# Binary cross-entropy on one core: target as u8, longer rows, one software DMA queue, a small first tile and a last tile in pieces

## The chip, the cores and the metric

The kernel runs on one core of a Trainium2 chip. The metric is the device time of one execution in microseconds (us), lower is better. Before the change it is 1882.6 us (median of 4 runs, 1882.17 to 1883.1).

## The reference

```python
pred   = uniform(0.01, 0.99, (8192, 8192)) as float32
target = randint(0, 2, (8192, 8192)) as float32      # 0.0 or 1.0
pred = clip(pred, 1e-7, 1 - 1e-7)
out  = -(target * log(pred) + (1 - target) * log(1 - pred))
```

Because target is 0 or 1, each output is one of two logarithms, negated. Both inputs and the output are 268.4 MB in DRAM, so 805.3 MB have to cross between DRAM and the core. No kernel here can avoid that.

## The kernel before

```python
W = n_cols                      # 8192
C = 2048
p_pool = tile_pool(bufs=4)      # [128, 8192] fp32
t_pool = tile_pool(bufs=4)      # [128, 8192] bf16
u_pool = tile_pool(bufs=2, space=PSUM)

for rb in range(num_row_blocks):            # 64
    # ... cut: allocation of p_tile and t_tile
    nc.gpsimd.dma_start(out=p_tile, in_=pred_f[r0:r1, :])
    nc.gpsimd.dma_start(out=t_tile, in_=target_f[r0:r1, :])   # casts fp32 to bf16
    for cb in range(num_chunks):            # 4 chunks of 2048
        # ... cut: c0, c1, u_tile
        nc.scalar.activation(u_tile, p_tile[:, c0:c1], LN, bias=0.0, scale=1.0)
        nc.scalar.activation(p_tile[:, c0:c1], p_tile[:, c0:c1], LN, bias=1.0, scale=-1.0)
        nc.vector.copy_predicated(out=p_tile[:, c0:c1],
                                  mask=t_tile[:, c0:c1].bitcast(i16), data=u_tile)
        nc.vector.tensor_scalar_mul(out=p_tile[:, c0:c1], in0=p_tile[:, c0:c1], scalar1=-1.0)
    nc.scalar.dma_start(out=out_f[r0:r1, :], in_=p_tile)
```

ScalarE makes log(pred) into PSUM, the second on-chip memory beside that of the tiles, and log(1 - pred) in place. VectorE overwrites the latter with the former where target is 1, then negates. The loads go through GpSimd's software queue, the stores through ScalarE's hardware queue.

## Time and profile before

| | before |
|---|---|
| span of the profiled execution | 1880.6 us |
| VectorE / ScalarE busy | 49% / 51% |
| DMA queues, share of 16 engines | 66.6% loads, 33.2% stores |
| one row's DMA record: pred / target / store | 1213 / 1227 / 1213 to 1226 ns |
| rate in the bulk, counted in DRAM bytes | 432.7 GB/s |
| DMA idle: first 10 us / after 1800 us | 2.8 / 13.8 us |

A row is what one DMA record of the trace moves: 8192 elements of one partition, 32,768 B on the DRAM side. The row times are the usual values of such records. The bulk is the stretch from 200 to 1800 us; its rate gives each row its DRAM bytes, spread over its record, in stretches of 150 us. Idle is the mean over 16 engines of the time with fewer than 16 records in flight, up to the end of the last record.

From the page of the kernel before: the DMA line of the 40-slice part (each digit is the busy share of a slice in tenths), the queues (packets, MB, share), and the engines and lines of the chain that ended last.

```profile
DVE 923.0 (49%) x512; ACT 951.5 (51%) x513; POOL 72.2 (4%) x132
...
DMA  9999999999999999999999999999999999999996
...
q0 software_dynamic: 18432, 402.66, 66.6%
q10 hardware_dynamic: 9216, 268.44, 33.2%
...
another core or an unknown queue 44%; ACT 38%; DVE 12%; issue 3%; DMA 2%; POOL 0%; ACTq 0%; DVEq 0%; PEldq 0%
```

DMA is saturated everywhere but in the last slice, and no compute engine is busy for more than 51% of the span. The two shares stand as 2 to 1, as the loads' DRAM bytes do to the stores'. The 402.66 MB of the first queue are written bytes, where target counts only half. So the time follows the side with more bytes.

The waits of the kernel before (engine, line, what was waited for: us in total, times, longest):

```profile
POOL p_tile L48 <- DMA out_dram<-p_tile: 1598.3, 56, 57.1
DVE p_tile L60 <- ACT p_tile L57: 834.4, 88, 14.8
ACT u_tile L56 <- DMA p_tile<-in_pred_dram: 799.2, 63, 14.6
```

Everybody waits for transfers: the loads for a store to free a buffer, ScalarE for pred, VectorE for ScalarE. These waits cost nothing while the DMA engines have work. What costs is where the engines run out of work. Two stretches of the kernel before, by engine busy time, clock, DMA share and GB/s (written bytes):

```profile
200.00:1800.00 1600.00, 795.16 (x441) 816.78 (x441) 58.57 (x109) 1.00 1.01 360
...
1845.00:1881.00 36.00, 14.66 (x8) 14.83 (x8) 0.00 (x0) 1.00 0.56 238
```

At the end, 0.44 of 36 us, 16 us, are idle, the last store's completion included. The timeline there (start, duration, instruction, idle before it and what ended it):

```profile
1839.54 1.23 DVE L63 TENSOR_SCALAR p_tile<-p_tile 128x2048 f32<-128x2048 f32 x1
1849.19 1.88 ACT L56 ACTIVATE u_tile<-p_tile 128x2048 f32<-128x2048 f32 x1 [12.71 <-DMA p_tile<-in_pred_dram]
1851.10 1.91 ACT L57 ACTIVATE p_tile<-p_tile 128x2048 f32<-128x2048 f32 x1
1851.11 0.34 ACTq L67 DMA_DIRECT2D out_dram<-p_tile  x1
...
1867.90 0.34 ACTq L67 DMA_DIRECT2D out_dram<-p_tile  x1
```

The next-to-last block is finished at 1840.8, but its store leaves ScalarE's queue at 1851.1, behind the first logarithm of the last block. The last store leaves at 1867.9, once all four chunks are done.

### The profile page before, as it was taken

The numbers are of one execution on the slowest core, as the hardware profiler recorded it, in microseconds if no ns is written. First come the engines' busy times: TensorE is split into PE (matmuls) and PEld (weight loads), VectorE is DVE, ScalarE is ACT, GpSimd is POOL, SyncE is SP. The second block draws the span as 40 slices with busy tenths as digits, with TensorE's granted clock in tenths as the row PEclk, the third lists the DMA queues.
The fourth block names the chain that finished last, engine by engine and source line by source line (L and its number), as shares of the span: only waits on it lengthen the run. The fifth ranks groups of instructions, "written<-read, shape, count | busy, mean of one in ns | idle before, by whom it ended". The sixth has DMA issues, their size and how long they took to land.

```text
span 1880.6 us, 1631 instructions
## 1 busy us (share of the span) xinstructions
DVE 923.0 (49%) x512; ACT 951.5 (51%) x513; POOL 72.2 (4%) x132
## 2 busy tenths in 40 slices
DVE  3545535446354464454544545536355354563544
ACT  4545545546445455464553644635446455464453
POOL 0000000000000000000000000000000000000000
DMA  9999999999999999999999999999999999999996
GB/s 309 373 357 351 338 356 373 345 377 356 351 378 345 365 366 347 384 344 355 378 343 375 355 350 383 344 363 370 343 382 350 351 381 345 370 361 346 385 345 286
DMA packets 27661, 671.21 MB, mean 357 GB/s; under 512 B 3072, under 2 KB 3072, under 8 KB 3072
## 3 DMA queue, kind: packets, MB, share of 16 engines
q0 software_dynamic: 18432, 402.66, 66.6%
q10 hardware_dynamic: 9216, 268.44, 33.2%
q14 instruction: 13, 0.11, 0.0%
HBM read 536.87 MB, written 268.44 MB: 428 GB/s over the span
## 4 chain that ended last, share of the span: by engine, by line
another core or an unknown queue 44%; ACT 38%; DVE 12%; issue 3%; DMA 2%; POOL 0%; ACTq 0%; DVEq 0%; PEldq 0%
ACT u_tile L56 20%; ACT p_tile L57 18%; DVE p_tile L60 11%; DMA t_tile<-in_target_dram 2%; DVE p_tile L63 1%; POOL p_tile L48 0%; ACTq L56 0%; POOL t_tile L49 0%; DVEq L60 0%; PEldq L93 0%
## 5 line engine op out<-in xcount | busy, mean ns | idle before, releaser
L60 DVE COPY_PREDICATED p_tile<-t_tile,u_tile 128x2048 f32<-128x2048 int16 x256 | 619.3, 2432 | 938.3 <-ACT p_tile L57 834.4
L56 ACT ACTIVATE u_tile<-p_tile 128x2048 f32<-128x2048 f32 x256 | 479.2, 1872 | 902.9 <-DMA p_tile<-in_pred_dram 799.2
L57 ACT ACTIVATE p_tile<-p_tile 128x2048 f32<-128x2048 f32 x256 | 484.9, 1906 | 9.0 <-DVE p_tile L63 2.9
L63 DVE TENSOR_SCALAR p_tile<-p_tile 128x2048 f32<-128x2048 f32 x256 | 310.6, 1224 | 6.6
L48 POOL DMA_DIRECT2D p_tile<-in_pred_dram x64 | 35.5, 555 | 1708.2 <-DMA out_dram<-p_tile 1598.3
L49 POOL DMA_DIRECT2D t_tile<-in_target_dram x64 | 37.3, 583 | 7.4 <-DVE p_tile L60 7.3
L56 ACT ACT_TABLE_LOAD x1 | 1.3, 1283 | 0.7 <-PEq L82 0.7
L82 POOL MEMSET const-float32-0.0<- 128x1 f32 x1 | 0.1, 98 | 0.2 <-issue 0.2
L82 POOL MEMSET const-bfloat16-1.0<- 128x1 bf16 x1 | 0.1, 101 | 0.0
L82 POOL MEMSET const-float32-1.0<- 128x1 f32 x1 | 0.1, 98 | 0.0
L82 POOL MEMSET const-uint8-127<- 128x1 uint8 x1 | 0.1, 98 | 0.0
## 6 DMA issues: line engine op xcount, KB each, us to landing
p_tile<-in_pred_dram POOLq DMA_DIRECT2D x64, 4096.0 KB, 61.6
out_dram<-p_tile ACTq DMA_DIRECT2D x64, 4096.0 KB, 23.1
t_tile<-in_target_dram POOLq DMA_DIRECT2D x64, 2048.0 KB, 75.7
```

Of the source, the lines that this page charges most:

```text
L48: nc.gpsimd.dma_start(out=p_tile, in_=pred_f[r0:r1, :])
L49: nc.gpsimd.dma_start(out=t_tile, in_=target_f[r0:r1, :])
L56: nc.scalar.activation(u_tile, p_tile[:, c0:c1], LN, bias=0.0, scale=1.0)
L57: nc.scalar.activation(p_tile[:, c0:c1], p_tile[:, c0:c1], LN, bias=1.0, scale=-1.0)
L60: nc.vector.copy_predicated(out=p_tile[:, c0:c1], mask=t_tile[:, c0:c1].bitcast(i16), data=u_tile)
L63: nc.vector.tensor_scalar_mul(out=p_tile[:, c0:c1], in0=p_tile[:, c0:c1], scalar1=-1.0)
L82: nc = _bacc.Bacc("TRN2", target_bir_lowering=False, num_devices=1)
```

## The change

Its intent is to move the same bytes in fewer, longer rows and to leave less work for the ends. The core of the diff, condensed (`...` and the comment lines stand for code that is cut, and some lines are shortened):

```diff
-    bf16 = mybir.dt.bfloat16
+    u8 = mybir.dt.uint8
-    C = 2048 if n_cols % 2048 == 0 else n_cols
+    CH = 1888
+    C = 8 * CH                                       # 15104: rows of 60,416 B
+    # flat view: widths = [1888] + [15104] * 34 + [8864], 36 tiles
-    p_pool = ... bufs=4;  t_pool = ... bufs=4;  u_pool = ... bufs=2 (2048 wide)
+    p_pool = ... bufs=3;  t_pool = ... bufs=2;  u_pool = ... bufs=1 (3776 wide)
+    # u_pool becomes bufs=2, 1888 wide, for the last two tiles
     ...
+    p_load_split(0, engine=nc.sync)                  # small first tile
+    t_load(0); p_load(1); t_load(1); p_load(2)       # all on gpsimd
+    for k in range(NT):
+        # chunks of 3776 (1888 in the last two tiles): ln, ln, copy_predicated, negate
-                out=p_tile[:, c0:c1], mask=t_tile[:, c0:c1].bitcast(i16), data=u_tile
+                out=p_tile[:, c0:c1], mask=t_tile[:, c0:c1], data=u_tile[:, 0:cw]
+            if last: nc.sync.dma_start(out=dr_out[:, c0:c1], in_=p_tile[:, c0:c1])
-        nc.scalar.dma_start(out=out_f[r0:r1, :], in_=p_tile)
+        store(k)                                     # on gpsimd
+        t_load(k + 2)
+        p_load(k + 3)
```

The loads, formerly issued at the head of each block and prefetched by the pools alone, are now placed by hand behind the store.

More of the change, by code (lines that the diff above doesn't have):

```diff
@@ L18 @@
     P = nc.NUM_PARTITIONS
+    fp32 = mybir.dt.float32
+    u8 = mybir.dt.uint8
+    LN = mybir.ActivationFunctionType.Ln
     pred_f = pred.flatten_outer_dims()
-    target_f = target.flatten_outer_dims()
-    out_f = out.flatten_outer_dims()
     n_rows, n_cols = pred_f.shape
-    assert n_rows % P == 0
-    fp32 = mybir.dt.float32
-    bf16 = mybir.dt.bfloat16
-    i16 = mybir.dt.int16
-    LN = mybir.ActivationFunctionType.Ln
-    W = n_cols
-    C = 2048 if n_cols % 2048 == 0 else n_cols
-    num_row_blocks = n_rows // P
@@ L35 @@
-    num_chunks = W // C
-    p_pool = ctx.enter_context(tc.tile_pool(name="p_pool", bufs=4))
-    t_pool = ctx.enter_context(tc.tile_pool(name="t_pool", bufs=4))
-    u_pool = ctx.enter_context(tc.tile_pool(name="u_pool", bufs=2, space=bass.MemoryType.PSUM))
-    for rb in range(num_row_blocks):
-        r0 = rb * P
-        r1 = r0 + P
-        p_tile = p_pool.tile([P, W], fp32)
-        t_tile = t_pool.tile([P, W], bf16)
-        nc.gpsimd.dma_start(out=p_tile, in_=pred_f[r0:r1, :])
-        nc.gpsimd.dma_start(out=t_tile, in_=target_f[r0:r1, :])
-        for cb in range(num_chunks):
-            c0 = cb * C
-            c1 = c0 + C
-            u_tile = u_pool.tile([P, C], fp32)
-            nc.scalar.activation(u_tile, p_tile[:, c0:c1], LN, bias=0.0, scale=1.0)
+    N = n_rows * n_cols
@@ new lines @@
+    assert N % P == 0
+    F = N // P
+    pf = pred.flatten()
+    tf = target.flatten()
+    of = out.flatten()
+    CH = 1888
+    C = 8 * CH
+    if F <= C:
+        C = F
+        CH = min(2048, C)
+        widths = [C]
+    else:
+        C0 = CH
+        rem = F - C0
+        n_full = rem // C
+        tail = rem - n_full * C
+        widths = [C0] + [C] * n_full + ([tail] if tail else [])
+    NT = len(widths)
+    offs = [0] * NT
+    for k in range(1, NT):
+        offs[k] = offs[k - 1] + P * widths[k - 1]
@@ new lines, with dram_tile_full @@
+    p_bufs = min(3, NT)
+    t_bufs = min(2, NT)
+    p_pool = ctx.enter_context(tc.tile_pool(name="p_pool", bufs=p_bufs))
+    t_pool = ctx.enter_context(tc.tile_pool(name="t_pool", bufs=t_bufs))
+    u_ctx = ExitStack()
+    u_pool = u_ctx.enter_context(tc.tile_pool(name="u_wide", bufs=1, space=bass.MemoryType.PSUM))
+    p_tiles: dict[int, object] = {}
+    t_tiles: dict[int, object] = {}
+    def dram_tile_full(flat_ap, k):
+        base = offs[k]
+        w = widths[k]
+        return flat_ap[base : base + P * w].rearrange("(p c) -> p c", c=w)
@@ new lines, in p_load, with p_load_split @@
+    def p_load(k, engine=None):
+        w = widths[k]
+        tl = p_pool.tile([P, C], fp32, name="ptile")
+        (engine or nc.gpsimd).dma_start(out=tl[:, 0:w], in_=dram_tile_full(pf, k))
+        p_tiles[k] = tl
+    def p_load_split(k, engine, p_split=32):
+        w = widths[k]
+        tl = p_pool.tile([P, C], fp32, name="ptile")
+        src = dram_tile_full(pf, k)
+        engine.dma_start(out=tl[0:p_split, 0:w], in_=src[0:p_split, :])
+        engine.dma_start(out=tl[p_split:P, 0:w], in_=src[p_split:P, :])
+        p_tiles[k] = tl
@@ new lines, in t_load, with store @@
+    def t_load(k):
+        w = widths[k]
+        tl = t_pool.tile([P, C], u8, name="ttile")
+        nc.gpsimd.dma_start(out=tl[:, 0:w], in_=dram_tile_full(tf, k))
+        t_tiles[k] = tl
+    def store(k):
+        w = widths[k]
+        eng = nc.gpsimd
+        eng.dma_start(out=dram_tile_full(of, k), in_=p_tiles[k][:, 0:w])
+    if NT > 1:
+        p_load_split(0, engine=nc.sync)
+    else:
+        p_load(0)
+    for b in range(min(t_bufs, NT)):
+        t_load(b)
+        if b + 1 < min(p_bufs, NT):
+            p_load(b + 1)
@@ new lines @@
+    for k in range(NT):
+        p_tile = p_tiles[k]
+        t_tile = t_tiles[k]
+        ck = widths[k]
+        last = k == NT - 1
+        dr_out = dram_tile_full(of, k) if last else None
+        if k == NT - 2:
+            u_ctx.close()
+            u_pool = ctx.enter_context(tc.tile_pool(name="u_pool", bufs=2, space=bass.MemoryType.PSUM))
+        cmax = CH if k >= NT - 2 else 2 * CH
+        c0 = 0
+        while c0 < ck:
+            cw = min(cmax, ck - c0)
+            c1 = c0 + cw
+            u_tile = u_pool.tile([P, cmax], fp32, name="utile")
+            nc.scalar.activation(
+                u_tile[:, 0:cw], p_tile[:, c0:c1], LN, bias=0.0, scale=1.0
+            )
@@ L65 @@
             )
-        nc.scalar.dma_start(out=out_f[r0:r1, :], in_=p_tile)
+            if last and NT > 1:
+                nc.sync.dma_start(out=dr_out[:, c0:c1], in_=p_tile[:, c0:c1])
+            c0 = c1
+        if last:
+            if NT == 1:
+                store(k)
+            break
+        store(k)
+        if k + t_bufs <= NT - 1:
+            t_load(k + t_bufs)
+        if k + p_bufs <= NT - 1:
+            p_load(k + p_bufs)
 _INS = ['pred', 'target']
```

## The prediction

> **What bounds the kernel now.** The DMA engines. The slice row has DMA at 9 in every slice but the last; the queue table gives 66.6% of 16 engines' span to the software queue (loads) and 33.2% to the hardware queue (stores); VectorE is busy 49%, ScalarE 51%. In the waits, loads wait 1598 us for stores to land, ScalarE 799 us for pred. The chain of waits names 44% an unknown queue, which I read as the same thing.
>
> The bytes that count are those of the wider side. In the DMA records a 32,768 B pred row takes 1213 ns, a target row (32,768 B read, 16,384 B bf16 written) 1227 ns, a store row 1213 to 1226 ns. So the cast's smaller output buys nothing. From 200 to 1800 us there are 23,790 packets, 2,651 of them tiny completions: 21,139 rows x 32,768 B in 1600 us = 433 GB/s. The Trainium skill, "DMA: Bandwidth & Descriptors", section Bandwidth ("Where 436 GB/s comes from"), puts the ceiling at 435 GB/s; this trace agrees, 0.5% under. The 805.3 MB at 433 GB/s are 1861 us; the other 20 us are ends: 2 us before the first packet, about 16 us idle in the last 36 us (DMA share 0.56 in the window 1845 to 1881), because the last two 4 MB stores wait for whole-tile compute.
>
> **What the change does.** Target becomes u8 (still 4 B read per element). Rows grow from 32,768 to 60,416 B, 192 transfers become about 113. All bulk transfers go on one software queue, in the order store k, target k+2, pred k+3; buffers fall to 3 and 2. PSUM has one 3776-wide buffer, so ScalarE and VectorE hardly overlap. The first tile is small; the last is stored in pieces on another queue.
>
> **Costs, estimated from the durations above.**
> - DMA: per-row overhead (1213 against 1205 ns at 27.2 B/ns, the skill's ceiling) is paid half as often: about -5 us. With one queue nothing hides the cast's 14 ns per row and the completions: 0 to +8 us. Bulk 1860 to 1870 us.
> - Compute per 15,104-wide tile: 4 serial chunks of ln 3.4 + ln 3.4 + predicated copy 4.4 us (scaled from 1.87, 1.91 and 2.43 us at 2048), plus the last negation 2.2: 47 us. DMA per tile: 3 x 7.73 MB at 433 GB/s = 54 us. Compute stays hidden, 13% spare. The pred load waits for its store to land, but an 18 us target load is queued between, so the engines do not run dry.
> - Tail: queued transfers cover the last compute; idle in the last 36 us falls from 16 to about 3 us. Start: no change.
>
> **Predicted time: 1870 us, 8 in 10 within 1861 to 1882.** Faster by over 2%: 3%; within 2%: 92%; slower by over 2%: 5%. At 435 GB/s 805.3 MB are 1851 us, so 2% (1845 us) is out of reach unless something else binds.
>
> **What would show each step.** HBM bytes unchanged (537 read, 268 written); row records of about 2230 ns for pred, 2240 to 2260 for target; DMA 9 in all slices, the last no longer 6; ScalarE waiting for VectorE's predicated copy, both still near 50% busy; load waits still ended by stores landing.
>
> **What would make it wrong.** The cast to u8 running slower than the read side (each extra 100 ns per target row costs about 28 us); a u8 mask slowing the predicated copy so that a tile's chain passes 54 us; the single queue draining at tile boundaries, or reads and writes in turn running below 433 GB/s.

## The result

The changed kernel takes 1866.65 us (median of 8 runs, 1865.46 to 1869.63), against 1882.43 us (13 runs) for the kernel before. The ratio is 0.9916 with a 95% interval of 0.9906 to 0.9926. A ratio here is the mean time of one kernel's runs over that of the other's of the same rounds, so it is not quite the ratio of the medians quoted. Executions over 1.5% slower than the fastest of the same kernel are left out of the means. The gain of 15.8 us is clear of noise.

| | before | after |
|---|---|---|
| span of the profiled execution | 1880.6 us | 1865.3 us |
| row record: pred / target | 1213 / 1227 ns | 2229 / 2244 ns |
| bulk rate, DRAM bytes | 432.7 GB/s | 433.9 GB/s |
| DMA idle: first 10 us / after 1800 us | 2.8 / 13.8 us | 1.9 / 4.0 us |

From the page of the changed kernel, the same parts:

```profile
DVE 897.7 (48%) x292; ACT 928.9 (50%) x293; POOL 57.0 (3%) x110
...
DMA  9999999999999999999999999999999999999998
...
q0 software_dynamic: 15264, 598.48, 99.3%
q1 hardware_dynamic: 880, 5.51, 0.8%
...
ACT 36%; DVE 34%; another core or an unknown queue 26%; DMA 2%; issue 1%; DVEq 0%; POOL 0%; PEldq 0%
```

Still saturated, now also in most of the last slice. The chain of waits names ScalarE and VectorE for 70% of the span, and the engines are not busier: a chain is one path back through releases, and its shares are not costs. (The experiments e11 and e12 show how far compute is from binding.)

The waits of the changed kernel:

```profile
POOL ptile L69 <- DMA out_dram<-ptile: 1574.8, 33, 49.0
ACT utile L116 <- DVE ptile L122: 892.6, 134, 15.5
DVE ptile L122 <- DMA ttile<-in_target_dram: 476.3, 34, 29.2
```

ScalarE waiting for VectorE's predicated copy is now 892.6 us, against 103.7 in the kernel before: with one PSUM buffer, the next logarithm can start only when the copy has read the last one. Two stretches of the changed kernel:

```profile
200.00:1800.00 1600.00, 771.62 (x240) 795.18 (x242) 48.10 (x90) 1.00 1.00 325
...
1829.00:1866.00 37.00, 15.21 (x10) 9.39 (x6) 0.00 (x0) 1.00 0.82 337
```

The DMA share at the end is 0.82 in place of 0.56: 7 us idle, not 16. The 325 against 360 GB/s of the bulk is not a slowdown. It counts written bytes, and u8 writes fewer. The end of the changed kernel's timeline shows what is in flight:

```profile
1824.03 0.54 POOL L89 DMA_DIRECT2D out_dram<-ptile  x1 [39.07 <-DVE ptile L125]
1825.37 1.78 ACT L119 ACTIVATE ptile<-ptile 128x1888 f32<-128x1888 f32 x1
1835.92 4.39 DVE L122 COPY_PREDICATED ptile<-ttile,utile 128x1888 f32<-128x1888 uint8 x2 [12.18 <-DMA ttile<-in_target_dram]
...
1849.29 1.88 DVE L125 TENSOR_SCALAR ptile<-ptile 128x1888 f32<-128x1888 f32 x2
```

The next-to-last store (7.7 MB, about 18 us of transfer) is issued at 1824, before the last target has landed (1835.9). In the queue it stands right behind that load, and it runs while the last tile is computed: by the DMA records 102 of its 128 rows end after 1835.9, the last one at 1854.

### The profile page after: what moved, and what is told of

It is laid out like the page before. It is cut to its first block, busy times and chain, and to the rows that moved or that the text cites. A ratio compares the mean times of both kernels' runs of the same rounds, so it can differ in the third digit from the quotient of the medians.

```text
span 1865.3 us, 922 instructions
## 1 busy us (share of the span) xinstructions
DVE 897.7 (48%) x292; ACT 928.9 (50%) x293; POOL 57.0 (3%) x110
## 4 chain that ended last, share of the span: by engine, by line
ACT 36%; DVE 34%; another core or an unknown queue 26%; DMA 2%; issue 1%; DVEq 0%; POOL 0%; PEldq 0%
DVE ptile L122 32%; ACT ptile L119 18%; ACT utile L116 18%; DMA ttile<-in_target_dram 2%; DVE ptile L125 2%; DVEq L122 0%; DVEq L167 0%; POOL ttile L83 0%; POOL ptile L69 0%; PEldq L167 0%
## 5 line engine op out<-in xcount | busy, mean ns | idle before, releaser
L122 DVE COPY_PREDICATED ptile<-ttile,utile 128x3776 f32<-128x3776 uint8 (+1 forms) x146 | 602.5, 4129 | 948.6 <-DMA ttile<-in_target_dram 476.3
L116 ACT ACTIVATE utile<-ptile 128x3776 f32<-128x3776 f32 (+1 forms) x146 | 462.2, 3166 | 907.5 <-DVE ptile L122 892.6
L119 ACT ACTIVATE ptile<-ptile 128x3776 f32<-128x3776 f32 (+1 forms) x146 | 466.3, 3195 | 4.5
L125 DVE TENSOR_SCALAR ptile<-ptile 128x3776 f32<-128x3776 f32 (+1 forms) x146 | 296.2, 2031 | 4.9
L69 POOL DMA_DIRECT2D ptile<-in_pred_dram x35 | 18.6, 532 | 1574.8 <-DMA out_dram<-ptile 1574.8
L89 POOL DMA_DIRECT2D out_dram<-ptile x35 | 18.8, 536 | 191.7 <-DVE ptile L125 191.7
L83 POOL DMA_DIRECT2D ttile<-in_target_dram x36 | 19.7, 548 | 0.8 <-PEq L167 0.8
```

The costliest lines, as they stand in the source:

```text
L69: (engine or nc.gpsimd).dma_start(out=tl[:, 0:w], in_=dram_tile_full(pf, k))
L83: nc.gpsimd.dma_start(out=tl[:, 0:w], in_=dram_tile_full(tf, k))
L89: eng.dma_start(out=dram_tile_full(of, k), in_=p_tiles[k][:, 0:w])
L116: nc.scalar.activation(u_tile[:, 0:cw], p_tile[:, c0:c1], LN, bias=0.0, scale=1.0)
L122: nc.vector.copy_predicated(out=p_tile[:, c0:c1], mask=t_tile[:, c0:c1], data=u_tile[:, 0:cw])
```

## The experiments

The theory was: 11 us of the gain are idle time at the ends (16.6 to 5.9 us in the table), 5 us are the longer rows, and u8 by itself and the choice of queue are worth nothing. Its rivals: fewer bytes written on chip, the single queue, the stores in pieces. All kernels gave correct results.

### e1: the kernel before, stores from SyncE

```diff
-        nc.scalar.dma_start(out=out_f[r0:r1, :], in_=p_tile)
+        nc.sync.dma_start(out=out_f[r0:r1, :], in_=p_tile)
```

> The kernel before with one edit: the stores are issued from SyncE, not from ScalarE's queue. Theory (the gain of the change is 11 us of idle at the ends and some 5 us of larger rows): in the kernel before, the next-to-last store, though its data were negated by 1840.8 us, left ScalarE's queue only at 1851.1, behind the next tile's logarithms; freed of that, about 5 us of the idle at the end go: 1877 us (1875 to 1879), DMA in the bulk unchanged at 433 GB/s. Rival 1 (the cast to u8 or the row size alone makes the gain): 1882 us, no change. Rival 2 (late stores cost all through the run): well below 1875 us.

Measured: 1883.45 us (1881.03 to 1885.61), ratio 1.0005 (0.999 to 1.002). This is a miss: 1875 to 1879 was expected. The stores do leave at once, but the idle after 1800 us grew from 13.8 to 16.7 us. The timeline of e1 at the end:

```profile
1841.76 3.68 ACT L56 ACTIVATE u_tile<-p_tile 128x2048 f32<-128x2048 f32 x2 [3.21 <-DMA p_tile<-in_pred_dram]
1845.38 3.69 ACT L57 ACTIVATE p_tile<-p_tile 128x2048 f32<-128x2048 f32 x2
1857.64 4.74 DVE L60 COPY_PREDICATED p_tile<-t_tile,u_tile 128x2048 f32<-128x2048 int16 x2 [14.90 <-DMA t_tile<-in_target_dram]
```

The DMA engines keep the same rate in the bulk (432.7 GB/s in e1 too), so a store that runs earlier pushes the last load later. The last target now lands at 1857.6. In the kernel before, the last load to land was pred, at 1849.2. After it only the last block is left, and the DMA engines idle through its 14 us of compute. What matters at the end is not how early a store goes, but how much is still queued when the last load lands.

### e2: e1, and the last block stored chunk by chunk

```diff
+            if rb == num_row_blocks - 1:
+                nc.sync.dma_start(out=out_f[r0:r1, c0:c1], in_=p_tile[:, c0:c1])
...
-        nc.scalar.dma_start(out=out_f[r0:r1, :], in_=p_tile)
+        if rb < num_row_blocks - 1:
+            nc.sync.dma_start(out=out_f[r0:r1, :], in_=p_tile)
```

> The kernel before, stores from SyncE, and the last row block stored in four pieces as each 2048-wide chunk is done. Theory: the end's idle falls by about 10 us in all, 1871.5 us (1869 to 1874): more than half of the change's 15.8 us, without u8, larger rows or a single queue. Rival (the gain is in the bulk of the transfers): no more than e1.

Measured: 1878.65 us (1876.41 to 1880.27), ratio 0.9983 (0.9966 to 1.0). The idle after 1800 us fell to 4.3 us as expected, but the time fell by 3.7 us, not 11, and lies outside the 1869 to 1874 expected: a miss in size. In the profiled execution (span 1874.6 us) the rate sags to 429 to 431 GB/s from 1400 to 1850 us, which costs some of what the end gains. The times themselves spread by 4 us, where the kernel before spreads by 1.3. In its mechanism at the end the theory holds. The sag was not foreseen, and its cause stays open; 186 rows of this run take over 5% more than usual, against 50 in the kernel before, and e7 has more of this.

### e3: the kernel before, target as u8

```diff
-        t_tile = t_pool.tile([P, W], bf16)
+        t_tile = t_pool.tile([P, W], mybir.dt.uint8)
...
-mask=t_tile[:, c0:c1].bitcast(i16)
+mask=t_tile[:, c0:c1]
```

> The kernel before with one edit: target is cast to u8 in place of bf16, a quarter of the read size is written in place of half. Theory (a transfer takes the time of its wider, read side): 1882 us (1881 to 1884), target rows 1227 ns as before, HBM bytes the same. Rival (bytes written to on-chip memory count): 67 MB fewer, at 433 GB/s some 150 us off, or a part of that.

Measured: 1881.45 us, ratio 0.9995 (0.998 to 1.001). A target row takes 1227 ns, as with bf16, though it writes 8192 B in place of 16,384. By itself u8 is worth nothing that is clear of the noise: the median is 0.9 us lower, and the interval contains 1. It makes room on chip: at the changed kernel's tile width, bf16 has one more byte for each target element, which over two buffers of 15,104 elements would add 30 KB per partition.

### e4 and e6: the changed kernel with the old row size

```diff
-    CH = 1888
+    CH = 1024
```

> The changed kernel with chunk width 1024 in place of 1888, so rows of 32,768 B as before, all else kept. Theory (each row of 16 engines pays 8 to 10 ns beside its bytes, whatever its size, and the target rows some 14 ns more): row records 1213 and 1227 ns, bulk longer by about 8 us against the changed kernel: 1874 us (1871 to 1878). Rival (row size is worth nothing; the single queue or the order of transfers makes the bulk faster): 1866.7 us, as the changed kernel.

Measured in e4: 1872.83 us, but spread from 1870.32 to 1880.93. The profiled execution was the slowest of the four, with a bulk rate down to 423 GB/s in the middle. It was run again beside the changed kernel itself (e5), on one chip, with more rounds.

> The changed kernel itself, unaltered, as the control for the other runs of this group on the same chip. Both theories: 1866.7 us (1865 to 1870), a ratio of 0.9916 to the kernel before.

Measured in e5: 1866.27 us (1865.45 to 1866.96), ratio 0.9911.

> The kernel of e4 again, because e4's four times spread from 1870 to 1881 us and the rate of its profiled run dips to 423 GB/s for some 300 us in the middle. Theory (larger rows lift the bulk rate from 432.8 to 433.9 GB/s, some 5 us): fastest runs 1870 us, 4 to 6 us over the changed kernel's fastest, and the target of 433 GB/s in a run without a dip. Rival (row size is worth nothing, e4's median was disturbance): within 2 us of the changed kernel.

Measured in e6: 1871.31 us (1870.81 to 1875.04), ratio 0.9944 (0.9932 to 0.9956). The fastest runs differ by 5.4 us and the medians by 5.0. Rows are 1213 and 1227 ns again. The last stretch of e6, as long as that of the changed kernel above (DMA share 0.82):

```profile
1835.00:1872.00 37.00, 19.35 (x21) 17.91 (x19) 0.54 (x1) 1.00 0.84 277
```

This splits the gain: against the kernel before, e6 gains 11.3 us (1882.66 - 1871.31) with the old row size, and its idle at the ends (1.9 and 3.9 us) is 10.8 us less. The longer rows give the other 5.0 us, together with the larger tiles and fewer transfers that come with them; no run separates these. The usual row durations, summed and shared over 16 engines, differ by more, 1871.0 against 1861.8 us, so some 4 us of them did not show in the time, and why is open.

### e7: the changed kernel with the bulk stores on SyncE's queue

```diff
-        eng = nc.gpsimd
+        eng = nc.sync
```

> The changed kernel with the bulk stores on SyncE's queue, so that there are two queues through the bulk as in the kernel before. Theory (which queue carries the bytes is worth next to nothing; ends and row size make the gain): within 3 us of the changed kernel. Rival (the single queue, in which loads and stores follow one another, makes the bulk faster): the bulk falls to 432.7 GB/s or less and the time rises by 5 us or more.

Measured: 1916.1 us, the median of five runs (1902.52 to 1925.77), ratio 1.0165 (1.0131 to 1.02): 50 us lost by one word. A sixth run, 1934.19 us, is slow and left out here; with it the median is 1918.14, the 52 us that the next expectations quote. The theory missed. The rival's forecast was met (5 us or more, and the bulk at 426.3 GB/s), but its size was foreseen by neither. The queues of the profiled execution (span 1900.8 us, its fastest) and its bulk:

```profile
q0 software_dynamic: 10224, 334.58, 66.6%
q1 hardware_dynamic: 5920, 269.40, 33.1%
...
200.00:1800.00 1600.00, 759.63 (x236) 780.78 (x235) 71.76 (x58) 1.00 1.00 321
```

The DMA engines are as busy as ever (1.00). The work itself takes longer. Against e5 the span is 35.6 us longer: 847 of 13,056 wide rows take over 5% more than the median of their kind (97 in e5), and the excess of these is 26.6 us per engine (1.7 in e5). The 99th percentile of the wide rows on GpSimd's queue is 3.4 us (2.34 in e5, where the stores are on it too). The idle at both ends is 6.4 us more. Sampled through the bulk, 1.9 to 2.2 rows are stretched at any time while a store and a pred load are both in flight, 0.2 to 0.9 while only loads are. The 50 us themselves were not profiled: the trace is of the fastest run.

### e8: the changed kernel, last tile stored whole

```diff
-            if last and NT > 1:
-                nc.sync.dma_start(out=dr_out[:, c0:c1], in_=p_tile[:, c0:c1])
...
+            nc.sync.dma_start(out=dr_out, in_=p_tile[:, 0:ck])      # after the last chunk
```

> The changed kernel with the last tile (8864 wide) stored by one transfer once all five chunks are done, not in five pieces. Theory (the end is covered because the 7.7 MB store before it is queued behind the last load and still runs while the last tile is computed, 1836 to 1851 us): within 2 us of the changed kernel, 1865 to 1869. Rival (the pieces cover the end): the last tile's 15 us of compute appear as idle, 5 to 12 us more.

Measured: 1866.82 us (1866.42 to 1868.61), ratio 0.9917. No difference from e5 at this resolution. The last stretch of e8 has a DMA share of 0.84, although its only remaining store is issued late:

```profile
1829.00:1866.00 37.00, 15.20 (x10) 9.39 (x6) 0.00 (x0) 1.00 0.84 338
```

```profile
1849.99 0.37 SPq L131 DMA_DIRECT2D out_dram<-ptile  x1
```

So the pieces are not what covers the end. The next-to-last store queued behind the last load is. e7 is the counter-test, though it was run for another reason: there this store has a queue of its own and runs beside the last load.

```profile
1858.61 0.33 SPq L89 DMA_DIRECT2D out_dram<-ptile  x1
1880.63 2.24 DVE L122 COPY_PREDICATED ptile<-ttile,utile 128x1888 f32<-128x1888 uint8 x1 [22.05 <-DMA ttile<-in_target_dram]
```

By 1880.6, when the last target has landed, 115 of its 128 rows have ended, against 26 by 1835.9 in the changed kernel, and the idle after 1800 us is 9.4 us, against 2.9 in e5.

### e9 and e10: does the second queue hurt only with long rows?

e9 is e7 with `CH = 1024` (32,768 B rows), e10 with `CH = 1536` (49,152 B rows).

> The kernel of e6 (the changed kernel with 32,768 B rows) with the bulk stores on SyncE's queue, the edit of e7. e7 lost 52 us to rows stretched from 2.23 us to as much as 3.4 us, most where a store and a pred load are in flight together. Theory A (two queues do this only with the long rows): no stretched rows, as in the kernel before, within 4 us of e6's 1871 us. Theory B (two queues in this order of transfers and with these buffers do it at any row size): 1900 us or more, as e7.

> As e9, with chunk width 1536, rows of 49,152 B, between the two. Theory A, if the stretching grows with row size: between e9 and e7's 1918 us, some 1885 to 1905. Theory A', if it is the odd pitch of 60,416 B and not the size (49,152 B is a multiple of 16,384): as e9, near 1870 us. Theory B: as e7.

Measured: e9 1903.55 us (1888.66 to 1906.18), ratio 1.0097 (1.0058 to 1.0135); e10 1926.44 us (1920.4 to 1930.3), ratio 1.0241. So it is neither the long row nor the pitch of 60,416 B. By the times theory B stands: in this order of transfers and with these buffers, a second queue hurts at any of the three sizes. That stretched rows are how it costs the time is seen in e7 and in e10 (1303 rows, 41.6 us per engine, beside 9.6 us of idle between 10 and 1800 us), not in e9: its profiled execution, its fastest, has 411, and the slowest run of e4, with one queue for the same rows, has 440. So a second queue is not needed for stretched rows. In e12 below, with one queue again, there are 1507, and 976 of them start within 2 us of a moment with fewer than 5 rows in flight. Two queues alone are not enough either, for the kernel before and e1 have two, and only 50 of their 24,576 rows are stretched. What in the order makes the difference stays open: the distance between the addresses read and written, or which engines are in which transfer. No run took these apart.

### e11 and e12: how much compute can be hidden

```diff
             nc.vector.copy_predicated(out=..., mask=..., data=...)
+            nc.vector.copy_predicated(out=..., mask=..., data=...)   # e12: every chunk; e11: every other
```

This is condensed: in e11 the second copy stands under an `if` for every other chunk. The result is the same, since the second copy repeats the first.

> The changed kernel with the predicated copy made twice for every other chunk (same result): the chain of a wide tile grows from 4 x 11.1 = 44.4 us to 53.1 us, just under the 53.5 us that its three transfers take at 433.9 GB/s. Theory (compute is hidden, with 9 us to spare per tile): no or little change, 1866 to 1880 us. Rival (compute is partly exposed already): some 34 x 8.7 = 296 us more, or a good part of it.

> The changed kernel with the predicated copy made twice for every chunk (same result): the chain of a wide tile becomes 4 x (11.1 + 4.35) = 61.8 us, over the 53.5 us of its transfers. Theory: the kernel turns compute bound, 33 wide tiles at 61.8 us after the first 44 us plus the last two tiles: 2150 us (2110 to 2190), and the DMA row shows gaps. Rival (chunks of neighbouring tiles overlap, so that the chain is no limit): below 1950 us.

Measured: e11 1866.56 us, e12 2163.04 us (one run each). From the bulk of e11 and of e12:

```profile
200.00:1800.00 1600.00, 1038.60 (x302) 804.43 (x244) 48.77 (x92) 1.00 1.00 325
```

```profile
200.00:1800.00 1600.00, 1118.26 (x311) 687.12 (x206) 79.28 (x78) 1.00 0.91 280
```

e11 adds 303 us of VectorE work and nothing that shows to the time (1866.27 in e5). Its chain of 53.1 us per tile still fits under the 53.5 us of transfer. e12's chain of 61.9 us does not, DMA falls to 0.91, and the kernel is compute bound. So compute does not bind the changed kernel, although its chain of waits names VectorE and ScalarE for 70%. In e11 it names them for 97%, at no cost:

```profile
DVE 49%; ACT 48%; DMA 2%; issue 1%; POOL 0%; DVEq 0%; PEldq 0%
```

## Why the prediction was right

- **Time.** 1870 us was predicted within 1861 to 1882, and 1866.65 was measured. "Within 2%" was given 92%, and it is.
- **The bound.** Right. DMA was saturated before and after. The bulk rates of 432.7 and 433.9 GB/s stand 0.6% and 0.3% under the 435 GB/s that the Trainium skill gives ("DMA: Bandwidth & Descriptors", section Bandwidth). At that figure the bytes take 1851 us, an estimate, and 2% less than before is 1845, so 2% was out of reach.
- **u8 buys nothing.** Right, shown alone in e3.
- **The end.** Idle "from 16 to about 3 us" was predicted for the last 36 us. It fell to 7 us in the last 37, the end of the last store included. As the DMA records have it, 13.8 became 4.0, so 9.8 us came where 12 to 13 were expected. The reason given, that queued transfers cover the last compute, is what e8 and the end of e7 show.
- **The start.** "No change" missed a small term: 0.9 us less idle. The first load now leaves SyncE's queue at 0.74 us; before, it left GpSimd's at 1.25.
- **Row overhead.** "About -5 us", measured 5.0 us between e6 and e5.
- **One queue.** "0 to +8 us" for a cast and completions that nothing hides. It was about 0: e6, one queue and old row size, has the bulk rate of the kernel before in its undisturbed stretches (432.6 to 433.2 against 432.7), and over its whole bulk 432.5. The middle of this term, 4 us, would account for the 3 us by which the centre was too high. The prediction worried about the single queue; in this order of transfers a second one was the danger.
- **Row records.** Predicted 2230 and 2240 to 2260 ns, measured 2229 and 2244.
- **Compute.** Predicted 47 us per tile under 54, "13% spare". Measured in the timeline: a chunk every 11.1 us, 44.4 us per tile. The last negation overlaps with the next tile, so the spare time is 17%. e11 used nearly all of it for nothing, and e12 went over.

## What to carry to other kernels

When the DMA engines are saturated, count the bytes of the wider side of each transfer; what is left to gain is the fixed time of each row and the idle at the two ends. At the end, ask what is still queued when the last load lands: a large store queued behind that load covers the last compute, and sending it earlier only moves the load later. Treat the choice of queue as something to measure, for one word cost more here (50 us) than the whole change gained.

## What the Trainium skill lacked or had wrong

- "DMA: Bandwidth & Descriptors", sections "Issuing engines are not separate DMA queues" and "Rules for kernel authors": they say that spreading transfers over issuing engines "Doesn't help", and saves only issue time. They lack that it can hurt. Moving the stores of the changed kernel from GpSimd's to SyncE's queue took it from 1866.3 to 1916.1 us (e7), with wide rows of the load queue at 3.4 in place of 2.34 us at the 99th percentile. e9 and e10 repeat the loss of time at two other row sizes; the kernel before, with two queues, has no such rows (50 of 24,576).
- The same page, section Bandwidth: one sentence says that for HBM-SBUF transfers the HBM side (about 358 GB/s) binds, while the page's own table, for a single core, has 425 GB/s for a load of 16 MB. Here, with the program on one core, 433 to 434 GB/s held over the whole bulk, loads and stores mixed. "HBM Reference", section Specifications (TRN2), gives about 425 for a core streaming alone, which is nearer.
- The same page, "Why small descriptors are slow": it gives a fixed cost of about 3 cycles a packet, with a 256 B descriptor as its case, and nothing for long rows. Here the records of plain rows of 7,552, 32,768 and 60,416 B (286, 1213, 2229 ns) lie on one line, 27.2 B/ns and 8 ns over. Going from 32 KB to 60 KB rows, with the larger tiles, saved 5.0 us of 1871.
- No page read here prices a cast in a DMA. A cast row takes 14 to 15 ns more than a plain one, at either row size and to bf16 or u8 alike (1227 against 1213, 2244 against 2229 ns), and nothing is gained from the smaller output.
